# Prompt tokens alone through the seven products, sample tokens through plain products in a bank of their own

## The chip, the cores and the metric

The kernel runs as one launch on one core of a Trainium2 chip. The metric is the device time of that launch in microseconds (us). Before the change it was measured three times: the median is 2774.99 us. A difference of about 0.2%, some 5.5 us, is the least that such a measurement can tell from no change.

## The reference, cut to what matters

One step of a two-layer encoder runs for 1024 prompt tokens and for 8 sample streams of 16 tokens, 1152 tokens in all, in fp32. Model width is 1024 and the channel mixer is 2 x 2816 wide. The part that the change touches is a product of all tokens with a weight matrix, in three places: the up-projection of both layers' channel mixers, and the keys that the second layer's attention shares.

```python
def conv_ffn(h, prev, w_up, conv_w, conv_b, w_down):
    u = h @ w_up                        # 1152 x 1024 times 1024 x 5632
    ...                                 # causal convolution of width 3 over positions
    a, g = jnp.split(y, 2, axis=-1)
    out = (jax.nn.gelu(g) * a) @ w_down
...
kv = ((x * (1 + sc_kv) + sh_kv) @ w_kv_b).reshape(B, T, 2, N_HEADS_B, HEAD_DIM)
```

## The kernel before, in words

Tokens lie along the free dimension of the transposed activations H: nine tiles of 128 tokens, tile 8 holding the samples. Each fp32 operand is split into two parts that TensorE takes in its fp32r format: hi is a cast by ScalarE (ACT) and lo is the rest, a subtraction by VectorE (DVE). The method is `split`, whose cast is at L180 and whose subtraction is at L191. A product of two split operands takes three matmuls per 128-deep slice: lo x hi, hi x lo and hi x hi.

The up-projection of a layer is made in 22 pairs of 128 columns (an "a" block and its gate "g"). The first two pairs of a layer are plain: 24 matmuls per block of about 384 tokens. The other 20 pairs, and four pairs of key columns between the layers, go through `products`, a Strassen-Winograd scheme: a 2 x 2 block product in seven block products, not eight. The token halves are the two 64-token halves of each tile, the depth halves are rows 0-511 and 512-1023, the column halves are the "a" and the "g" block. GpSimd (POOL) makes the sums of weights (L1174 to L1177); `tsums` makes the sums of token blocks once per stage (POOL L1133 and DVE L1134 and L1135, then splits), for all nine tiles, into areas that are 576 = 9 x 64 tokens wide. The names of these areas in the profile are xa, x2r and, for the fourth sum in the key stage, wh and wl.

Each of the seven products is 128 columns x 576 half tokens, cut by `NB` into 320 and 256 tokens in two neighbouring banks of PSUM (the accumulator, 512 fp32 per partition and bank): 12 matmuls with 320 moving columns and 12 with 256 (L1226), 168 in a pair. In a matmul the weight part is the stationary operand, loaded anew for each one (PEld in the profile, as many as matmuls); the tokens move. Products are read out by ACT or DVE at L1185, L1187 and L1194, then added into the rows ua and ug of the pair, and the convolution and the gate follow (`conv_row`, `conv_row_psum`, `gated`). The products of a pair accumulate in three groups of banks: 11 and 21 in group 0; 2, 3 and 4 in group 1; 1 and 22 in group 2. A product that continues a group has to wait until the one before has been read out.

The order of the products is (11, 2, 21, 3, 1, 4, 22). It is (11, 21, 22, 2, 3, 1, 4) in the first pair of a stage, since 11, 21 and 22 need no token sums, and (11, 2, 3, 1, 4, 21, 22) in the last pair of keys. Split weights live in a ring of half slots: eight in layer 0, six in layer 1, three in the key stage. A scheduler orders the instructions of each engine from the written order and the dependencies; it moves whole groups of matmuls ahead where it expects an operand to be late. In layer 0 small matmuls of the modulation (`ada`, L237) run between products. After the second layer's pairs come the down-projections (L1476 in layer 0, L1600 in layer 1) and, elsewhere, products of tokens as the stationary operand (`mmX`, L322).

On-chip memory is laid out by pools in this order: H, the weight slots wh and wl, ws, F, a small area C of 1840 fp32 per partition, then X1 (xa), X2 (x2r) and w0 (w0r). 1840 x 4 bytes is no multiple of 256, all other sizes are. So xa, x2r and w0r start 192 bytes past a multiple of 256, while H, wh and wl start at one.

Of the kernel before, what the change touches and what calls it, by code (L numbers as in the profile page):

```python
# [10 lines left out]
F32 = mybir.dt.float32  # L11
# [24 lines left out]
NPL = 2  # L36
# [69 lines left out]
class Trunk:  # L106
    def __init__(self, ctx, tc, I, O):
# [4 lines left out]
        nc = self.nc  # L112
        mem = ctx.enter_context(tc.tile_pool(name="mem", bufs=1))
# [9 lines left out]
        ws = mem.tile([128, 2, 1024], F32, name="ws")  # L123
# [715 lines left out]
    def kv(self, hmring):  # L839
        nc, I, O, H, F = self.nc, self.I, self.O, self.H, self.F  # L840
# [3 lines left out]

        def T1(p, ks, n):
            m = NB[n][3] - NB[n][2]
            if ks.start < 3:
                return body[p][:, 0:1728].rearrange("p (k n) -> p k n", k=3)[:, ks, NB[n][2] : NB[n][3]]
            x = self.wslots[1][p][:, 512 : 512 + m] if n else body[p][:, 1728 : 1728 + m]
            return x.unsqueeze(1)  # L850

        T1S = F[:, 6180:8484].rearrange("p (k t i) -> p k t i", k=4, i=64)
        TT = self.tviews() + [T1]
        p1s = [F[:, 8484:8804], F[:, 8804:9060]]
# [29 lines left out]
        w = vload(0, self.wslots)  # L884
# [3 lines left out]
        for t in order:  # L888
            vtile(0, t, w, banks.next())
        self.tsums(raws, order, T1S, TT)  # L890

# [9 lines left out]

        sub = Ring(self.subslots(self.wslots[0:2]).items[0:3])
        narrow = self.ws
        wide = Ring(narrow.items + [F[:, o : o + 1024] for o in (3876, 4900)])
        for m in range(4):
            sa, sg = wide.next(), wide.next()
            nc.sync.dma_start(sa, I["wk1"][2 * m])
            nc.sync.dma_start(sg, I["wk1"][2 * m + 1])
            ua, ug = us.next(), us.next()

            def after(i, q, m=m, ug=ug):
                if q == 4:
                    kout(2 * m + 1, ug)

            self.products(sa, sg, ua, ug, S, p1s, sub, TT, after, {0: "first", 3: "last"}.get(m))
            kout(2 * m, ua)
# [206 lines left out]
    def tsums(self, ring, order, T1S, TT):  # L1123
        nc = self.nc
        E = nc.vector if len(TT) == 4 else nc.gpsimd
        for t in order:
            s = ring.next()
            nc.sync.dma_start(s, self.hD[t])
            s4 = s.rearrange("p (c h i) -> p c h i", h=2, i=64)
            b11, b12, b21, b22 = s4[:, 0:4, 0], s4[:, 0:4, 1], s4[:, 4:8, 0], s4[:, 4:8, 1]  # L1130
            x1 = T1S[:, :, t, :]
            E.tensor_sub(x1, b12, b11)
            E.tensor_sub(b12, b22, b12)  # L1133
            nc.vector.tensor_sub(b22, b22, x1)  # L1134
            nc.vector.tensor_sub(b21, b21, b22)  # L1135
            c = slice(64 * t, 64 * t + 64)
            for src, (hi, lo) in zip((b22, b12, b21), TT):
                self.split(src, hi[:, :, c], lo[:, :, c], "a", "v")
            if len(TT) == 4:
                n = t // 5  # L1140
                c = slice(64 * t - 320 * n, 64 * t - 320 * n + 64)
                for ks in (slice(0, 3), slice(3, 4)):
                    hi, lo = (TT[3](p, ks, n)[:, :, c] for p in range(2))
                    self.split(T1S[:, ks, t, :], hi, lo, "a", "v")
        if len(TT) == 3:
            H5 = self.H.rearrange("p a c (t h i) -> p a c t h i", h=2, i=64)
            self.split(T1S, H5[:, 0, 0:4, :, 1, :], H5[:, 1, 0:4, :, 1, :], "a", "v")
# [6 lines left out]
    def products(self, sa, sg, ua, ug, S, p1s, sub, TT, after, when=None):  # L1154
        nc = self.nc
        H5 = self.H.rearrange("p a c (t h i) -> p a c t h i", h=2, i=64)

        def operand(q):
            if q in (2, 3, 4):
                t = TT[q - 2]  # L1160
                return lambda p, k, n: t[p][:, k, NB[n][2] : NB[n][3]]
            if q == 1 and len(TT) == 4:
                return lambda p, k, n: TT[3](p, slice(k, k + 1), n)[:, 0, :]
            c0, h = {11: (0, 0), 21: (4, 0), 22: (4, 1), 1: (0, 1)}[q]
            return lambda p, k, n: H5[:, p, c0 + k, NB[n][0] : NB[n][1], h, :]

        def halves(u, h, n):
            v = u[:, 2 + NB[n][0] * 128 : 2 + NB[n][1] * 128]
            return v.rearrange("p (t h i) -> p t h i", h=2, i=64)[:, :, h, :]

# [8 lines left out]
        def read(d, a, ps, n):  # L1179
            def v(x):  # L1180
                x = x[:, 0 : NB[n][3] - NB[n][2]]
                return x.rearrange("p (t i) -> p t i", i=64)

            if a is None:
                nc.scalar.copy(d, v(ps))  # L1185
            else:
                nc.vector.tensor_add(d, v(ps), a if len(a.shape) == 3 else v(a))  # L1187

        def evict(q, ps, n):
            p1 = p1s[n]  # L1190
            a0, a1, g0, g1 = (halves(u, h, n) for u in (ua, ug) for h in range(2))
            early = when == "first"
            if q == 11:
                nc.scalar.copy(p1, ps[:, 0 : NB[n][3] - NB[n][2]])  # L1194
            elif q == 21:
                read(a0, None, ps, n)
            elif q == 22:
                d = a1 if not early else p1
                read(a1, d, ps, n)
            elif q == 2:  # L1200
                d = a1 if early else p1
                read(a1, d, ps, n)
            elif q == 3:
                read(g1, p1, ps, n)
            elif q == 4:
                read(g0, p1, ps, n)
            else:
                read(g1, g1, ps, n)
                if early:
                    read(a1, a1, ps, n)  # L1210

# [3 lines left out]
        for i, q in enumerate(order):  # L1215
            w = sub.next()
            self.split(src[q], *w, "a", "v")
            x = operand(q)
            start = q in (11, 2, 1) or (q == 22 and when == "first")
            for n in range(2):  # L1220
                m = NB[n][3] - NB[n][2]
                ps = self.bank(2 * group[q] + n)
                c = 0
                for a, p in ((1, 0), (0, 1), (0, 0)):
                    for k in range(4):
                        self.pairmm = nc.tensor.matmul(  # L1226
                            ps[:, 0:m],
                            w[a][:, k * 128 : k * 128 + 128],
                            x(p, k, n),
                            start=start and c == 0,  # L1230
                            stop=c == 11,
                            skip_group_check=True,
                        ).ins
                        c += 1
                evict(q, ps, n)
            after(i, q)
# [4 lines left out]
    def ffn(self, l, xsrc, xdst, affs):  # L1241
# [21 lines left out]
        S1, S2, S3 = [F[:, o : o + 512] for o in (0, 512, 1024)]  # L1263
        p1s = [F[:, 9724:10044], F[:, 10044:10300]]
        T1S = F[:, 2706 : 2706 + 2304].rearrange("p (k t i) -> p k t i", k=4, i=64)
# [4 lines left out]
        cb, sb = Ring([6, 7]), Ring([1, 3, 5])  # L1270
        UB = ((0, 384), (380, 388), (764, 388))
# [48 lines left out]
        def conv_row_psum(u, j, gg, y):  # L1320
# [4 lines left out]
                x.rearrange("p (s q) -> p s q", q=16)  # L1325
                for x in (self.bank(sb.next())[:, 320:448], y[:, 1024:1152], u[:, 1026:1154])
            )
# [61 lines left out]
        def spair(j):  # L1389
# [18 lines left out]

            self.products(sa, sg, ua, ug, (S1, S2, S3), p1s, sub, TT, after, "first" if j == NPL else None)
            ya = yact if l else ys.next()  # L1410
# [10 lines left out]
        if l == 0:  # L1421
            self.bg = [self.ada(g, 7, wide) for g in (3, 4, 5, 6)]
        self.tsums(Ring([F[:, 1536:2560], F[:, 8700:9724], F[:, 11644:12668]]), (0, 1, 2, 3, 4, 8, 5, 6, 7), T1S, TT)
        for u in us.items:
# [632 lines left out]
```

## Time and profile before

| | us |
|---|---|
| median of three runs (lowest to highest) | 2774.99 (2771.91 to 2775.78) |
| the profiled execution's own time | 2778.73 |
| its span from the first to the last instruction | 2776.9 |
| TensorE matmul (PE) busy | 2656.2 (96%) |
| VectorE (DVE) busy | 1916.0 (69%) |
| ScalarE (ACT) busy | 1348.0 (49%) |
| GpSimd (POOL) busy | 1065.7 (38%) |

The 44 pairs run at 532 to 1013 us (layer 0), 1368 to 1466 us (keys) and 2042 to 2503 us (layer 1). In the profile PE is the matmul, PEld the load of a matmul's stationary operand. A matmul's recorded time runs from its start to the end of its results, so neighbours overlap. What a matmul costs in a stream is the distance from its start to the next start: in the timeline, where equal neighbours are merged into one row with their count, it is the start of the next row less the start of this one, divided by the count. A row's second column is the time from its first start to its last end.

### The profile page before, as it was taken

To read this page: it belongs to the slowest core of one execution; us is meant where nothing else is said; L and a number is where in the kernel's file an instruction comes from. 1 tells how busy PE (TensorE), PEld (TensorE's weight loads), DVE (VectorE), ACT (ScalarE), POOL (GpSimd) and SP (SyncE) were. 2 spreads that over 40 slices of the span, in tenths; PEclk is the share of its full clock that TensorE was granted. 3 is DMA by queue.
4 is the path that set the end of the run, shared out by engine and by line. 5 is a ranking of instruction groups with operands and counts; after the bars stand their busy time and mean duration, and the time that the engine had idled before them with its cause. 6 is when DMAs were issued, how large, how long until landed. Compare 5 with 4: busy or idle time off the path is not lost.

```text
span 2776.9 us, 47111 instructions
## 1 busy us (share of the span) xinstructions
PE 2656.2 (96%) x17266; PEld 2345.9 (84%) x17266; DVE 1916.0 (69%) x3836; ACT 1348.0 (49%) x2777; POOL 1065.7 (38%) x775
## 2 busy tenths in 40 slices
PE   7999889999999999999999999989999999999997
PEld 5987768989999998888898888867899999997776
DVE  4376767776666684767754667766787777785669
ACT  3475723433334343443536666662454445454454
POOL 3132623444434357664220121242466656632101
PEclk9999999999999999999999999989999999999999
DMA  7756434464444446765757457773544443347564
GB/s 289 236 162 193 145 103 167 163 236 148 139 158 147 147 135 220 240 217 182 277 192 263 121 155 195 213 213 115 176 143 173 144 138 135 136 148 246 189 221 155
DMA packets 229527, 498.27 MB, mean 179 GB/s; under 512 B 37456, under 2 KB 99232, under 8 KB 229296
## 3 DMA queue, kind: packets, MB, share of 16 engines
q1 hardware_dynamic: 229296, 495.27, 54.6%
q8 instruction: 136, 2.23, 0.3%
q14 instruction: 95, 0.78, 0.1%
HBM read 378.15 MB, written 126.47 MB: 182 GB/s over the span
## 4 chain that ended last, share of the span: by engine, by line
PE 38%; DVE 6%; DMA 4%; ACT 2%; issue 1%; POOL 0%; SPq 0%; DVEq 0%; ACTq 0%; POOLq 0%
PE PS L1226 18%; PE PS L1600 5%; PE PS L322 5%; PE PS L309 4%; PE PS L605 2%; PE PS L583 2%; DMA xa<-actD 1%; PE PS L554 1%; DVE xa L191 1%; DVE F L521 1%; DVE wl L191 1%; PE PS L557 1%; DMA xa<-actS 1%; PE PS L732 0%; DMA wl<-wT 0%
## 5 line engine op out<-in xcount | busy, mean ns | idle before, releaser
L1226 PE MATMUL PS<-H,wh 128*128 128x256 f32 (+1 forms) x2288 | 355.8, 296 | 0.0
L1187 DVE TENSOR_TENSOR F<-PS,F 128x256 f32<-128x256 f32 (+1 forms) x446 | 197.9, 453 | 182.1 <-PE PS L1226 172.7
L1226 PEld LDWEIGHTS PS<-H,wh 128*128 128x128 f32 x2288 | 322.6, 190 | 0.4 <-issue 0.4
L180 ACT CAST wh<-F 128x512 fp32r<-128x512 f32 (+3 forms) x241 | 147.7, 624 | 212.5 <-PE PS L1226 105.5
L191 DVE TENSOR_TENSOR wl<-F,wh 128x512 fp32r<-128x512 f32 (+2 forms) x225 | 213.4, 960 | 40.6 <-ACT wh L180 38.4
L1226 PE MATMUL PS<-H,wl 128*128 128x256 f32 (+1 forms) x1144 | 202.0, 297 | 6.2 <-ACT F L1194 6.2
L1600 PE MATMUL PS<-wh,xa 128*128 128x512 f32 x584 | 187.8, 398 | 14.6 <-ACT wh L180 7.6
L1226 PEld LDWEIGHTS PS<-H,wl 128*128 128x128 f32 x1144 | 168.6, 189 | 12.1 <-ACT F L1194 6.4
L1226 PE MATMUL PS<-xa,wh 128*128 128x320 f32 (+1 forms) x1152 | 175.2, 293 | 0.0
L180 ACT CAST xa<-xa 128x384 fp32r<-128x384 f32 (+2 forms) x143 | 85.8, 604 | 176.0 <-DMA xa<-actD 149.6
L1226 PEld LDWEIGHTS PS<-xa,wh 128*128 128x128 f32 x1152 | 159.0, 188 | 0.4 <-issue 0.4
L1469 DVE TENSOR_TENSOR xa<-xa 128x384 fp32r<-128x384 f32 x66 | 94.4, 1441 | 83.4 <-ACT xa L180 83.3
L1600 PEld LDWEIGHTS PS<-wh,xa 128*128 128x128 f32 x584 | 110.3, 190 | 44.3 <-ACT wh L180 11.8
L180 ACT CAST wh<-ws 128x512 fp32r<-128x512 f32 (+1 forms) x131 | 95.5, 736 | 101.4 <-PE PS L1226 44.2
L643 POOL TENSOR_TENSOR F<-F,x2r 64x512 f32<-64x512 f32 x62 | 79.4, 1280 | 165.9 <-DVE F L619 149.3
L1346 POOL TENSOR_TENSOR F<-F 128x1152 f32<-128x1152 f32 x44 | 124.1, 2820 | 43.9 <-DVE F L1339 18.1
L322 PE MATMUL PS<-xa,H 128*128 128x512 f32 x504 | 133.5, 406 | 6.2 <-ACT xa L180 3.3
L309 PE MATMUL PS<-H,w0r 128*128 128x384 f32 (+1 forms) x720 | 136.1, 340 | 0.0
L1275 DVE SCALAR_TENSOR_TENSOR F<-F 128x1024 f32<-128x1024 f32 (+2 forms) x160 | 132.1, 876 | 3.1 <-ACT F L1314 2.1
L309 PE MATMUL PS<-H,wh 128*128 128x384 f32 (+1 forms) x672 | 131.1, 338 | 0.0
L583 PE MATMUL PS<-C,F 128*128 128x128 f32 x720 | 112.7, 281 | 14.5 <-DVE wh L590 5.8
L309 PEld LDWEIGHTS PS<-H,w0r 128*128 128x128 f32 x720 | 123.2, 188 | 2.8 <-issue 1.1
(354 smaller groups left out, 6883.8 us busy)
## 6 DMA issues: line engine op xcount, KB each, us to landing
ws<-in_adaw_dram SPq DMA_DIRECT2D x64, 512.0 KB
ws<-in_wup_dram SPq DMA_DIRECT2D x49, 512.0 KB
F<-in_adaw_dram SPq DMA_DIRECT2D x48, 512.0 KB
F<-in_wup_dram SPq DMA_DIRECT2D x39, 512.0 KB
actD<-F SPq DMA_DIRECT2D x33, 576.0 KB
ws<-in_wdn_dram SPq DMA_DIRECT2D x33, 512.0 KB
F<-in_wdn_dram SPq DMA_DIRECT2D x33, 512.0 KB
xa<-kH SPq DMA_DIRECT2D x60, 256.0 KB
```

The lines of the kernel that those rows point to most:

```text
L180: nc.scalar.copy(out, in_)
L191: self.eng(el).tensor_sub(lo, src, hi.bitcast(F32))
L309: mm = self.nc.tensor.matmul(out[:, 0:n], w[a][:, k * 128 : k * 128 + 128], H[:, p, k, s0 : s0 + n], start=i == 0, stop=i == 23)
L322: self.nc.tensor.matmul(out[:, 0:n], H[:, p, j * kn + k, t0 : t0 + 128], w[a][:, k * n : k * n + n], start=i == 0, stop=i == 23,)
L583: nc.tensor.transpose(t[:, n * 128 : n * 128 + 128], p[:, (kt - k0) * 128 : (kt - k0) * 128 + 128], self.ident)
L643: self.eng("v" if last else "p").tensor_mul(on[r, q], on[r, q], rb[r, :])
L1187: nc.vector.tensor_add(d, v(ps), a if len(a.shape) == 3 else v(a))
L1226: self.pairmm = nc.tensor.matmul(ps[:, 0:m], w[a][:, k * 128 : k * 128 + 128], x(p, k, n), start=start and c == 0, stop=c == 11, skip_grou ...
L1275: nc.vector.scalar_tensor_tensor(o, u, cw[:, cc, i : i + 1], o, op0=ALU.mult, op1=ALU.add)
L1346: nc.gpsimd.tensor_mul(yg, yg, ya)
L1469: nc.vector.tensor_sub(lo, raw, hi.bitcast(F32))
L1600: self.downmm = nc.tensor.matmul(ps, a[p][:, i * 128 : i * 128 + 128], w[q], start=first and c == 0, stop=last and c == 2, skip_group_chec ...
```

## The change

The seven products now take the 1024 prompt tokens alone: 512 half tokens, a full bank, in 12 matmuls per product in place of 24. The areas of token sums are 512 wide, `tsums` runs over eight tiles, and the groups are banks 0, 1 and 2. The 128 sample tokens get their two output blocks by plain products: 8 depth slices x 3 matmuls for each of "a" and "g", 48 matmuls with 128 moving columns per pair, in bank 3 or 4 by turns. They use the split weights that the products have anyway (11, 21 and 4); only the plain block a21 has to be split in addition, before POOL overwrites it with a sum. ACT copies the two sample blocks out. The key stage's ring has four half slots in place of three. C grows by 16 fp32 per partition, so that xa, x2r and w0r start at a multiple of 256 bytes as H, wh and wl do.

```diff
-NB = ((0, 5, 0, 320), (5, 9, 320, 576))
...
-        C = mem.tile([128, 1840], F32, name="C")
+        C = mem.tile([128, 1856], F32, name="C")
...
-        sub = Ring(self.subslots(self.wslots[0:2]).items[0:3])
+        sub = self.subslots(self.wslots[0:2])
+        sbanks = Ring([3, 4])
...
-        TT = [(X1[:, 0:2304], X1[:, 2304:4608]), (X1[:, 4608:6912], X1[:, 6912:9216]), (X2[:, 0:2304], X2[:, 2304:4608])]
+        TT = [[x[:, o : o + 2048] for o in (i, i + 2048)] for x, i in ((X1, 0), (X1, 4096), (X2, 0))]
...
         E.tensor_sub(S3, a11, a21)
+        ws = sub.next()
+        self.split(a21, *ws, "a", "v")
         E.tensor_sub(a21, a12, S2)
...
+        def sample(b, w, c0, start=False):
+            n = slice(128 * b, 128 * b + 128)
+            i = 0
+            for a, p in ((1, 0), (0, 1), (0, 0)):
+                for k in range(4):
+                    nc.tensor.matmul(
+                        su[:, n],
+                        w[a][:, k * 128 : k * 128 + 128],
+                        H[:, p, c0 + k, 1024:1152],
+                        start=start and i == 0,
+                        stop=b in done and i == 11,
+                        skip_group_check=True,
+                    )
+                    i += 1
+            if b in done:
+                nc.scalar.copy((ua, ug)[b][:, 1026:1154], su[:, n])
+            done.add(b)
...
-            for n in range(2):
-                m = NB[n][3] - NB[n][2]
-                ps = self.bank(2 * group[q] + n)
-                c = 0
-                for a, p in ((1, 0), (0, 1), (0, 0)):
-                    for k in range(4):
-                        self.pairmm = nc.tensor.matmul(
-                            ps[:, 0:m],
-                            w[a][:, k * 128 : k * 128 + 128],
-                            x(p, k, n),
...
+            ps = self.bank(group[q])
+            c = 0
+            for a, p in ((1, 0), (0, 1), (0, 0)):
+                for k in range(4):
+                    self.pairmm = nc.tensor.matmul(
+                        ps,
+                        w[a][:, k * 128 : k * 128 + 128],
+                        x(p, k),
...
+            evict(q, ps)
+            if q == 11:
+                sample(0, w, 0, True)
+                sample(1, ws, 0)
+            elif q in (21, 4):
+                sample(q % 3, w, 4)
```

TensorE's order in a steady pair of layer 0. In the rows "H,w0r" means: tokens from H move, the weight slot w0r is loaded; L237 is the modulation. Before, products 11, 2 and 21 of one pair:

```order
L1226 MATMUL PS<-H,w0r 128x320 x12
L1226 MATMUL PS<-H,w0r 128x256 x12
L237 MATMUL PS<-F,C 32x256 x4
L1226 MATMUL PS<-xa,w0r 128x320 x12
L1226 MATMUL PS<-xa,w0r 128x256 x12
L1226 MATMUL PS<-H,wl 128x320 x4
L1226 MATMUL PS<-H,wh 128x320 x8
L1226 MATMUL PS<-H,wl 128x256 x4
L1226 MATMUL PS<-H,wh 128x256 x8
```

And of the changed kernel, products 11, 2 and 21 of such a pair (L1231 are the products, L1206 the samples):

```order
L1231 MATMUL PS<-H,w0r 128x512 x12
L1206 MATMUL PS<-H,w0r 128x128 x24
L1231 MATMUL PS<-xa,wl 128x512 x4
L1231 MATMUL PS<-xa,wh 128x512 x8
L1231 MATMUL PS<-H,wl 128x512 x4
L1231 MATMUL PS<-H,wh 128x512 x8
L1206 MATMUL PS<-H,wl 128x128 x4
L1206 MATMUL PS<-H,wh 128x128 x8
```

A run of 24 sample matmuls now stands behind product 11 and a run of 12 behind product 21; the last 12 stand around product 4. Over the whole program the 2112 sample matmuls stand in 172 runs.

The first pair of layer 1 on TensorE, behind the last plain block (128x388). Before:

```order
L309 MATMUL PS<-H,wh 128x388 x16
L1226 MATMUL PS<-H,wl 128x320 x4
L1226 MATMUL PS<-H,wh 128x320 x8
L1226 MATMUL PS<-H,wl 128x256 x4
L1226 MATMUL PS<-H,wh 128x256 x8
L1226 MATMUL PS<-H,wl 128x320 x4
L1226 MATMUL PS<-H,wh 128x320 x8
```

And changed:

```order
L308 MATMUL PS<-H,wh 128x388 x16
L1231 MATMUL PS<-H,wl 128x512 x4
L1231 MATMUL PS<-H,wh 128x512 x8
L1206 MATMUL PS<-H,wl 128x128 x4
L1206 MATMUL PS<-H,wh 128x128 x8
L1206 MATMUL PS<-H,wl 128x128 x4
L1206 MATMUL PS<-H,wh 128x128 x8
L1231 MATMUL PS<-xa,wl 128x512 x4
L1231 MATMUL PS<-xa,wh 128x512 x8
L1231 MATMUL PS<-H,wl 128x512 x4
L1231 MATMUL PS<-H,wh 128x512 x8
```

Product 11 was followed by another product over H in the same banks; now 24 sample matmuls and a product over token sums (xa) stand between the two.

More of the change, by code (lines that the diff above doesn't have):

```diff
@@ L843, in kv @@
         body = [self.w2[a][:, 1:3].rearrange("p s c -> p (s c)") for a in range(2)]
-        def T1(p, ks, n):
-            m = NB[n][3] - NB[n][2]
[L847 to L854, printed above, removed]
+        T1S = F[:, 6180:8228].rearrange("p (k t i) -> p k t i", k=4, i=64)
+        TT = self.tviews() + [[x.rearrange("p (k n) -> p k n", k=4) for x in body]]
+        p1 = F[:, 8484:8996]
         hl = [F[:, o : o + 1024].bitcast(F32R) for o in (9060, 10084)]
@@ L889, in kv @@
             vtile(0, t, w, banks.next())
-        self.tsums(raws, order, T1S, TT)
+        self.tsums(raws, [t for t in order if t < 8], T1S, TT)
         def kout(c, u):
@@ L913, in after @@
                     kout(2 * m + 1, ug)
-            self.products(sa, sg, ua, ug, S, p1s, sub, TT, after, {0: "first", 3: "last"}.get(m))
+            self.products(sa, sg, ua, ug, S, p1, sub, TT, sbanks.next(), after, {0: "first", 3: "last"}.get(m))
             kout(2 * m, ua)
@@ L1139, in tsums, with products, halves @@
             if len(TT) == 4:
[L1140 to L1144, printed above, removed]
+                hi, lo = TT[3]
+                self.split(T1S[:, :, t, :], hi[:, :, c], lo[:, :, c], "a", "v")
         if len(TT) == 3:
             H5 = self.H.rearrange("p a c (t h i) -> p a c t h i", h=2, i=64)
-            self.split(T1S, H5[:, 0, 0:4, :, 1, :], H5[:, 1, 0:4, :, 1, :], "a", "v")
+            self.split(T1S, H5[:, 0, 0:4, 0:8, 1, :], H5[:, 1, 0:4, 0:8, 1, :], "a", "v")
     def tviews(self):
         X1, X2 = self.X1, self.X2
-        TT = [(X1[:, 0:2304], X1[:, 2304:4608]), (X1[:, 4608:6912], X1[:, 6912:9216]), (X2[:, 0:2304], X2[:, 2304:4608])]
+        TT = [[x[:, o : o + 2048] for o in (i, i + 2048)] for x, i in ((X1, 0), (X1, 4096), (X2, 0))]
         return [[x.rearrange("p (k n) -> p k n", k=4) for x in t] for t in TT]
-    def products(self, sa, sg, ua, ug, S, p1s, sub, TT, after, when=None):
+    def products(self, sa, sg, ua, ug, S, p1, sub, TT, sbank, after, when=None):
         nc = self.nc
-        H5 = self.H.rearrange("p a c (t h i) -> p a c t h i", h=2, i=64)
+        H = self.H
+        H5 = H.rearrange("p a c (t h i) -> p a c t h i", h=2, i=64)
         def operand(q):
[L1159 to L1163, printed above, removed]
+            if q in (2, 3, 4) or (q == 1 and len(TT) == 4):
+                t = TT[(q - 2) % 4]
+                return lambda p, k: t[p][:, k, :]
             c0, h = {11: (0, 0), 21: (4, 0), 22: (4, 1), 1: (0, 1)}[q]
[L1165 to L1169, printed above, removed]
+            return lambda p, k: H5[:, p, c0 + k, 0:8, h, :]
+        def halves(u, h):
+            return u[:, 2:1026].rearrange("p (t h i) -> p t h i", h=2, i=64)[:, :, h, :]
         S1, S2, S3 = S
@@ L1325, in conv_row_psum @@
                 x.rearrange("p (s q) -> p s q", q=16)
-                for x in (self.bank(sb.next())[:, 320:448], y[:, 1024:1152], u[:, 1026:1154])
+                for x in (self.bank(sb.next())[:, 0:128], y[:, 1024:1152], u[:, 1026:1154])
             )
@@ L1407, in after @@
                     row(ug, j, 1, y[0])
-            self.products(sa, sg, ua, ug, (S1, S2, S3), p1s, sub, TT, after, "first" if j == NPL else None)
+            self.products(sa, sg, ua, ug, (S1, S2, S3), p1, sub, TT, sbanks.next(), after, "first" if j == NPL else None)
             ya = yact if l else ys.next()
@@ L1422, in ffn @@
             self.bg = [self.ada(g, 7, wide) for g in (3, 4, 5, 6)]
[L1423 removed]
+        self.tsums(Ring([F[:, 1536:2560], F[:, 8700:9724], F[:, 11644:12668]]), range(8), T1S, TT)
         for u in us.items:
```

46 lines of the change are left out of this document (21 added, 25 removed).

## The prediction

> **What bounds the kernel now.** First the page, for the engine that has no time to spare; then the windows of the stretch in which pair follows pair; then the timeline of TensorE, for what one matmul costs from start to start.
>
> ```profile
> span 2776.9 us, 47111 instructions
> PE 2656.2 (96%) x17266; PEld 2345.9 (84%) x17266; DVE 1916.0 (69%) x3836; ACT 1348.0 (49%) x2777; POOL 1065.7 (38%) x775
> ...
> PE PS L1226 18%; PE PS L1600 5%; PE PS L322 5%; PE PS L309 4%; PE PS L605 2%; PE PS L583 2%; DMA xa<-actD 1%; PE PS L554 1%; DVE xa L191 1%; DVE F L521 1%; DVE wl L191 1%; PE PS L557 1%; DMA xa<-actS 1%; PE PS L732 0%; DMA wl<-wT 0%
> ```
>
> TensorE is busy for 96% of the span, and L1226, the seven products, is the largest line of the chain that ends last. The windows (us, then busy time of PE, PEld, DVE, ACT, POOL) say whether anybody is waited for there. This stretch of layer 1 holds 16 pairs:
>
> ```profile
> 2117.60:2472.40 354.80, 354.79 (x2690) 354.57 (x2689) 269.86 (x469) 179.43 (x356) 223.93 (x170) 1.00 0.40 140
> ```
>
> PE has no idle time at clock 1.00; DVE has a quarter of it free, ACT half. A pair takes 354.80 / 16 = 22.18 us, and only PE's stream sets it. Layer 0 shows a pair without modulation, of which these are the start, three products and the next start:
>
> ```profile
> 968.52 0.83 PE L1226 MATMUL PS<-H,wl 128*128 128x320 f32 x4
> ...
> 971.80 3.35 PE L1226 MATMUL PS<-xa,w0r 128*128 128x320 f32 x24
> 974.99 3.34 PE L1226 MATMUL PS<-H,w0r 128*128 128x320 f32 x24
> 978.16 0.75 PE L1226 MATMUL PS<-xa,wl 128*128 128x320 f32 x4
> 978.75 1.34 PE L1226 MATMUL PS<-xa,wh 128*128 128x320 f32 x8
> 979.92 0.62 PE L1226 MATMUL PS<-xa,wl 128*128 128x256 f32 x4
> ...
> 990.80 0.75 PE L1226 MATMUL PS<-H,wl 128*128 128x320 f32 x4
> ```
>
> The pair takes 990.80 - 968.52 = 22.28 us, a product 3.17 to 3.19. A matmul of 320 columns costs 146 ns ((979.92 - 978.75) / 8), so one of 256 costs (3.18 - 12 x 0.146) / 12 = 119 ns. I take 22.2 us per pair, 44 times.
>
> **The products at 512 columns.** No product runs so in this trace, but other lines do:
>
> ```profile
> 1266.88 8.32 PE L1476 MATMUL PS<-x2r,xa 128*128 128x512 f32 x36
> 1275.04 0.40 PE L1476 MATMUL PS<-wh,xa 128*128 128x512 f32 x1
> ...
> 1945.24 5.76 PE L322 MATMUL PS<-xa,H 128*128 128x512 f32 x24
> 1950.84 0.39 PE L322 MATMUL PS<-wh,H 128*128 128x512 f32 x1
> ```
>
> Where both operands lie in areas with the same remainder modulo 256 bytes (x2r and xa), a matmul costs 8.16 / 36 = 227 ns; where they differ by 192 (xa and H), 5.60 / 24 = 233 ns. After the change all are alike. I take 228, a little over the better row for changes between areas; the bounds are 227 and 233. A product becomes 12 x 0.228 = 2.74 us, seven of them 19.15 us, against 22.2: a gain of 3.05 us per pair.
>
> **The samples at 128 columns.** 48 matmuls per pair, each with its own weight load. The rows with such matmuls in fp32r are in the first layer's attention (L605, four of them, then L309), and as transposes at L1039:
>
> ```profile
> 130.83 0.44 PE L605 MATMUL PS<-wh,xa 128*128 128x128 f32 x3
> 130.89 0.50 PE L605 MATMUL PS<-wh,xa 128*128 128x128 f32 x3
> 130.94 0.30 PEld L605 LDWEIGHTS PS<-wh,xa 128*128 128x128 f32 x2
> 131.23 0.56 PE L309 MATMUL PS<-H,w0r 128*128 128x384 f32 x2
> ...
> 1939.30 1.04 PE L1039 MATMUL PS<-C,F 128*128 128x128 f32 x8
> 1940.10 0.71 PE L322 MATMUL PS<-xa,H 128*128 128x512 f32 x2
> ```
>
> The two L605 rows are overlapping views of one run. The first matmul, behind a long one, hands over after 130.89 - 130.83 = 0.06 us. From there it is three steps to 131.23, 0.113 us each. The weight load of a step starts at 130.94, only after the matmul before it had started at 130.89: with 128 columns there is no long matmul in whose shadow the load can lie, so load and stream alternate. The eight transposes have the same step, 0.8 us for seven steps and a handover. I take 111 ns inside a run and 58 for the first of a run. The bounds are 58 (every load hidden) and 115.
>
> Samples of a pair in four runs: 44 x 0.111 + 4 x 0.058 = 5.12 us. A pair becomes 19.15 + 5.12 = 24.27 us, 2.07 more than 22.2. Times 44: **+91 us**. In columns alone the change is nearly even (7 x 12 x 576 = 48384 before, 7 x 12 x 512 + 48 x 128 = 49152 after); the loss is that 48 short matmuls cost their weight load too.
>
> The Trainium skill has another price ("TensorE: Matmul & The Clock Gate", Back-to-back issue gap): a sustained stream of load and matmul is said to take about 81 ns each at 128 columns and about 131 at 512. By these figures a pair would take 84 x 0.131 + 48 x 0.081 = 14.9 us, an estimate; the 227 ns of the row above already speaks against the second figure.
>
> **First pairs of the stages.** Before the 44 pairs run freely, PE waits for the token sums (its idle time stands in brackets with what ended it):
>
> ```profile
> 541.15 4.75 PE L1226 MATMUL PS<-H,w0r 128*128 128x320 f32 x24 [2.42 <-ACT F L1194]
> ...
> 1379.33 0.85 PE L1226 MATMUL PS<-xa,w0r 128*128 128x320 f32 x4 [1.07 <-ACT xa L180]
> 1382.09 2.89 PE L1226 MATMUL PS<-xa,w0r 128*128 128x320 f32 x20 [1.92 <-DVE xa L191]
> 1385.79 0.85 PE L1226 MATMUL PS<-wh,wl 128*128 128x320 f32 x4 [0.81 <-DVE F L1187]
> 1394.27 3.46 PE L1226 MATMUL PS<-x2r,w0r 128*128 128x320 f32 x24 [1.84 <-DVE F L1187]
> ...
> 2051.54 1.43 PE L1226 MATMUL PS<-H,wl 128*128 128x320 f32 x4 [6.18 <-ACT F L1194]
> 2052.78 2.33 PE L1226 MATMUL PS<-H,wh 128*128 128x320 f32 x8
> ```
>
> In both layers product 21 waits until ACT has read out 11, and ACT comes to that late, behind this cast of the last sum:
>
> ```profile
> 2047.46 2.11 ACT L180 CAST H<-F 128x2304 fp32r<-128x2304 f32 x1
> ```
>
> After the wait PE also runs slow for a while (2.33 us for eight matmuls that take 1.34 elsewhere). Behind product 11 there now stand 24 sample matmuls, 2.6 us of work that needs no sums, and in layer 1 a product over xa; the cast has 2048 columns, not 2304, and one tile of nine less is summed. I take layer 0's wait and its slow matmuls as gone (2.4 + 1.4), 7 us of layer 1's 6.2 + 2.3, and 3 us of the keys' 5.6. Together **-14 us**, between -4 and -20. What is late next there is the DVE, whose splits of the sums the product over xa awaits.
>
> **The places modulo 256 bytes.** Lines outside the pairs with 512 columns and unlike areas gain at most 233 - 227 = 6 ns each:
>
> ```profile
> L322 PE MATMUL PS<-xa,H 128*128 128x512 f32 x504 | 133.5, 406 | 6.2 <-ACT xa L180 3.3 <-DVE xa L191 1.5 <-DVE F L521 1.1
> L322 PE MATMUL PS<-w0r,H 128*128 128x512 f32 x162 | 44.0, 406 | 3.0 <-DVE F L1118 3.0
> L1600 PE MATMUL PS<-wh,xa 128*128 128x512 f32 x584 | 187.8, 398 | 14.6 <-ACT wh L180 7.6 <-DVE F L1729 2.8 <-DVE xa L191 2.3
> ```
>
> (504 + 162) x 6 ns = 4 us, and some 4 us more for the x2r rows of L322 and for L1600 and L1476, where the step already lies nearer to the good one. **-8 us**, between 0 and -12.
>
> **What costs nothing.** ACT, DVE and POOL work beside PE. The durations for it, from the same 16 pairs:
>
> ```profile
> L191 DVE TENSOR_TENSOR wl<-F,wh 128x512 fp32r<-128x512 f32 x81 | 78.1, 968 | 8.9 <-ACT wh L180 7.9 <-POOL F L1360 0.3 <-DMA ws<-in_wup_dram 0.2
> L1275 DVE SCALAR_TENSOR_TENSOR PS<-F,PS 128x512 f32<-128x512 f32 x65 | 48.5, 750 | 9.1 <-ACT PS L1337 9.1
> L1187 DVE TENSOR_TENSOR F<-PS,F 128x320 f32<-128x320 f32 x80 | 38.9, 486 | 10.8 <-PE PS L1226 8.9
> L1187 DVE TENSOR_TENSOR F<-PS,F 128x256 f32<-128x256 f32 x81 | 34.1, 420 | 39.8 <-PE PS L1226 36.6 <-ACT F L1194 3.0
> L180 ACT CAST wh<-F 128x512 fp32r<-128x512 f32 x81 | 50.1, 621 | 56.9 <-PE PS L1226 56.3
> ```
>
> DVE gets one split more, 0.97 us, and reads five products in one piece (0.75, the nearest row) in place of two (0.49 + 0.42): 0.97 - 5 x 0.16 = +0.2 us on 16.9 per pair. ACT gets a cast (0.62) and two sample copies (under 0.5 each), on 11.2. Both stay under the longer pair's 24 us. POOL's last weight sum now waits for the split of a21, with the next pair's sums and the gate's product queued behind it; it feeds product 22, seventh in order, some 18 us later. One bank per group means that the read-out (0.75 us and a handover) no longer hides under the other half of the same product; but between 2 and 3 stands 21, between 3 and 4 stands 1, each 2.74 us. Where that cover failed, one such wait per pair would cost 0.9 x 44 = 40 us. On SP's queue nothing is added and one tile load of nine per stage goes; weight loads get more time per pair.
>
> **Sum.** +91 - 14 - 8 = +69 us. The profiled execution took 2778.73 us, so 2848 by its own time; the median of the runs lies 3.7 lower, 2775 + 69 = **2844 us**.
>
> **Rivals.** (A) *Faster: the loads hide.* If PE loads ahead throughout, each sample matmul costs the 58 ns of a run's first: 48 x 0.058 = 2.8 us, a pair 21.95, -0.25 x 44 = -11, with -14 - 8 in all -33: 2742 us. It decides below (22.2 - 19.15) / 48 = 64 ns per sample matmul. For it: the first step of L605. Against it: every later one, and the transposes. 5%. (B) *Half of the loads hide*, 85 ns on average between 58 and 111: 4.1 us, a pair 23.2, +1.03 x 44 = +45, in all +23: 2798 us. Beside it stands the skill's 81 ns for 128 columns, the same page and section; no row here shows such a step. 6%. (C) *Read-outs come late*: the one-bank wait above once per pair, or ACT held up at the sample copies behind the next casts: +40 on the forecast, 2884 us. Against it: the order and ACT's free half. 7%. (D) *The longer matmul gives nothing beyond what 233 ns gives*: 84 x 5 ns x 44 = +18, 2862; within the range.
>
> **Chances and range.** The forecast, with D, has 82%. Its bounds: the 512 step -4 to +18, the sample step -15 (104 ns, if some runs are broken up) to +8, first pairs -6 to +10, places -4 to +8. Taken together 2815 to 2880; the range for 8 in 10 reaches down to B: 2802 to 2880. About 0.2%, 5.5 us, is what a measurement can tell from no change: faster 0.05 (A), the same 0.02 (between A and B), slower 0.93.
>
> **What would show it.** In the changed profile L1231 should step by 227 to 233 ns and L1206 by about 111 inside a run; a steady pair of layer 1 should take 24.3 us with PE busy throughout; the wait of 6.18 us at product 21 of layer 1 should be mostly gone. It is wrong if L1206 steps by 60 ns, if PE shows idle time before L1231 inside the steady pairs, or if a pair takes 22 us.

## The result, and the profile after

| | before | after |
|---|---|---|
| median, us (lowest to highest, four runs each) | 2775.38 (2771.91 to 2775.78) | 2865.91 (2862.35 to 2869.55) |
| the profiled execution's own time, us | 2778.73 | 2869.55 |
| its span, us | 2776.9 | 2867.8 |

The ratio is 1.0329, 95% interval 1.031 to 1.0348: the changed kernel is slower by some 90 us. The forecast was 2844, with a range of 2802 to 2880. (Of the four runs of before, three are those known ahead.) The page of the changed kernel, for the engine that sets the time:

```profile
span 2867.8 us, 43709 instructions
PE 2755.7 (96%) x15682; PEld 2299.8 (80%) x15682; DVE 1904.1 (66%) x3630; ACT 1377.0 (48%) x2802; POOL 1068.3 (37%) x771
...
PE PS L1231 28%; PE PS L321 11%; PE PS L1206 7%; PE PS L308 7%; PE PS L1486 7%; PE PS L1610 4%; PE PS L604 2%; PE PS L582 2%; PE PS L236 2%; PE PS L553 1%; DMA ws<-in_adaw_dram 1%; DMA F<-xd 1%; PE PS L295 1%; PE PS L556 1%; PE PS L731 1%
```

TensorE has 1584 matmuls fewer, is busy for the same 96% of the span, and is busy for 99.5 us longer. The samples' line, L1206, has entered the chain of work that ended last with 7%. Nobody else has become the bound. Steady pairs of layer 1 in the windows view (us; busy time of PE, PEld, DVE, ACT, POOL; granted clock), 13 of them:

```profile
2199.97:2519.77 319.80, 319.80 (x1717) 274.62 (x1716) 227.65 (x326) 151.86 (x300) 186.59 (x139) 1.00 0.36 127
```

A pair takes 319.80 / 13 = 24.60 us in place of 22.18, with PE busy throughout. The same view of the two kernels gives the lengths of the stages. Each is cut where the last matmul of a stage is done; where a few matmuls of the next stage stand ahead of it, they are counted with the next. (Layer 0's pairs end at 1036 us in the kernel before, not at 1013.)

| stage | before | after | difference |
|---|---|---|---|
| up to layer 0's pairs | 532.3 | 531.6 | -0.7 |
| 20 pairs of layer 0 | 503.8 | 552.9 | +49.1 |
| down-projection 0 and what follows | 332.4 | 339.7 | +7.3 |
| 4 pairs of keys | 96.9 | 102.6 | +5.7 |
| attention of layer 1 | 576.6 | 573.3 | -3.3 |
| 20 pairs of layer 1 | 452.6 | 493.5 | +40.9 |
| down-projection 1 and the end | 282.3 | 274.2 | -8.1 |
| span | 2776.9 | 2867.8 | +90.9 |

The pairs hold +95.7 us, and all the rest together -4.8. Inside a steady pair, TensorE's timeline of the changed kernel (start, length, line, operands, count) shows product 11's 24 sample matmuls, product 2, product 21 and its 12 samples:

```profile
2178.11 0.56 PE L1206 MATMUL PS<-H,wl 128*128 128x128 f32 x4
2178.50 1.06 PE L1206 MATMUL PS<-H,wh 128*128 128x128 f32 x8
2179.40 0.61 PE L1206 MATMUL PS<-H,wl 128*128 128x128 f32 x4
2179.85 1.06 PE L1206 MATMUL PS<-H,wh 128*128 128x128 f32 x8
2180.74 1.16 PE L1231 MATMUL PS<-xa,wl 128*128 128x512 f32 x4
2181.74 2.00 PE L1231 MATMUL PS<-xa,wh 128*128 128x512 f32 x8
2183.57 1.07 PE L1231 MATMUL PS<-H,wl 128*128 128x512 f32 x4
2184.48 1.98 PE L1231 MATMUL PS<-H,wh 128*128 128x512 f32 x8
2186.29 0.56 PE L1206 MATMUL PS<-H,wl 128*128 128x128 f32 x4
2186.68 1.06 PE L1206 MATMUL PS<-H,wh 128*128 128x128 f32 x8
2187.58 1.16 PE L1231 MATMUL PS<-xa,wl 128*128 128x512 f32 x4
```

A long matmul steps by (2186.29 - 2184.48) / 8 = 226 ns, as forecast. A sample matmul inside a run steps by (2180.74 - 2179.85) / 8 = 111 ns, as forecast too, and the first of a run is short: (2178.50 - 2178.11) / 4 = 97 ns on average for four with the first among them. What the forecast didn't have stands behind the run: the first four long matmuls take 2181.74 - 2180.74 = 1.00 us, where four others (2183.57 to 2184.48) take 0.91. A run gets back at its end what it saved at its head, so 24 samples cost 2.63 + 0.09 = 2.72 us, 113 ns each.

Now the first pairs of the stages, where the kernel before waited 6.18 us in layer 1, 2.42 in layer 0 and 5.64 in the quoted rows of the keys. These are the waits there in the timeline of after, with one at the end of layer 0 (idle time in brackets, with what ended it):

```profile
541.08 2.08 PE L1231 MATMUL PS<-H,wl 128*128 128x512 f32 x4 [3.59 <-ACT F L1182]
...
567.02 1.40 PE L1231 MATMUL PS<-x2r,wl 128*128 128x512 f32 x4 [1.30 <-DVE F L1176]
...
1021.31 1.67 PE L1231 MATMUL PS<-xa,wl 128*128 128x512 f32 x4 [1.76 <-DVE F L1176]
...
1448.73 2.08 PE L1231 MATMUL PS<-x2r,wl 128*128 128x512 f32 x4 [2.65 <-DVE F L1176]
...
2117.93 1.18 PE L1231 MATMUL PS<-H,wl 128*128 128x512 f32 x4 [1.32 <-DVE F L1176]
```

Layer 1's wait is mostly gone and the keys' are halved. Layer 0's has grown, and the wait at 1021.31, near the end of layer 0's pairs, is new. Behind most of these waits TensorE's clock is down for some 3 to 5 us, as the windows of after show at the keys' wait:

```profile
1448.73:1452.10 3.37, 3.37 (x8) 2.68 (x9) 2.22 (x3) 0.00 (x0) 0.47 (x1) 0.53 0.15 51
```

Eight matmuls take 3.37 us at a granted clock of 0.53. The down-projection of layer 0 now starts with two waits as well, in the timeline of TensorE and then of ACT:

```profile
1089.17 1.66 PE L1486 MATMUL PS<-wh,xa 128*128 128x512 f32 x6 [1.06 <-ACT wh L179]
...
1094.31 0.80 PE L1486 MATMUL PS<-wl,xa 128*128 128x512 f32 x1 [2.81 <-POOL wl L190]
```

```profile
1087.13 1.05 ACT L179 CAST xa<-ws 128x1024 fp32r<-128x1024 f32 x1 [3.16 <-DMA ws<-in_wdn_dram]
```

A weight tile lands late there, the cast of it starts late, and POOL's splits come late behind the cast. Behind the second wait the granted clock is 0.50 for 5.3 us.

### The profile page after: what moved, and what is told of

It reads as the page before. It is cut to its first block, busy times and chain, and to the rows that moved or that the text cites. A ratio compares the mean times of both kernels' runs of the same rounds, so it can differ in the third digit from the quotient of the medians.

```text
span 2867.8 us, 43709 instructions
## 1 busy us (share of the span) xinstructions
PE 2755.7 (96%) x15682; PEld 2299.8 (80%) x15682; DVE 1904.1 (66%) x3630; ACT 1377.0 (48%) x2802; POOL 1068.3 (37%) x771
## 4 chain that ended last, share of the span: by engine, by line
PE 78%; DMA 9%; DVE 7%; ACT 3%; issue 2%; POOL 1%; SPq 0%; DVEq 0%; ACTq 0%; POOLq 0%
PE PS L1231 28%; PE PS L321 11%; PE PS L1206 7%; PE PS L308 7%; PE PS L1486 7%; PE PS L1610 4%; PE PS L604 2%; PE PS L582 2%; PE PS L236 2%; PE PS L553 1%; DMA ws<-in_adaw_dram 1%; DMA F<-xd 1%; PE PS L295 1%; PE PS L556 1%; PE PS L731 1%
## 5 line engine op out<-in xcount | busy, mean ns | idle before, releaser
L1231 PE MATMUL PS<-H,wh 128*128 128x512 f32 x1184 | 294.1, 390 | 0.0
L1176 DVE TENSOR_TENSOR F<-PS,F 128x512 f32<-128x512 f32 x223 | 153.1, 688 | 192.3 <-PE PS L1231 191.5
L190 DVE TENSOR_TENSOR wl<-F,wh 128x512 fp32r<-128x512 f32 (+1 forms) x244 | 231.3, 965 | 69.8 <-ACT wh L179 68.4
L1231 PEld LDWEIGHTS PS<-H,wh 128*128 128x128 f32 x1184 | 222.6, 188 | 47.6 <-issue 0.4
L179 ACT CAST wh<-F 128x512 fp32r<-128x512 f32 (+2 forms) x260 | 162.8, 640 | 161.1 <-PE PS L1231 99.1
L1231 PE MATMUL PS<-xa,wh 128*128 128x512 f32 x672 | 168.5, 393 | 0.0
L1231 PE MATMUL PS<-H,wl 128*128 128x512 f32 x592 | 163.0, 397 | 4.9 <-ACT F L1182 3.6
L1231 PEld LDWEIGHTS PS<-xa,wh 128*128 128x128 f32 x672 | 127.1, 189 | 29.2
L1206 PE MATMUL PS<-H,wh 128*128 128x128 f32 x1016 | 138.4, 273 | 0.0
L1206 PEld LDWEIGHTS PS<-H,wh 128*128 128x128 f32 x1016 | 127.9, 192 | 2.3
L1231 PEld LDWEIGHTS PS<-H,wl 128*128 128x128 f32 x592 | 108.3, 189 | 26.7 <-ACT F L1182 3.7
```

The costliest lines, as they stand in the source:

```text
L179: nc.scalar.copy(out, in_)
L190: self.eng(el).tensor_sub(lo, src, hi.bitcast(F32))
L1206: nc.tensor.matmul(su[:, n], w[a][:, k * 128 : k * 128 + 128], H[:, p, c0 + k, 1024:1152], start=start and i == 0, stop=b in done and i == 11,
L1231: self.pairmm = nc.tensor.matmul(ps, w[a][:, k * 128 : k * 128 + 128], x(p, k), start=start and c == 0, stop=c == 11, skip_group_check=Tru ...
```

## The experiments

All kernels are edits of the changed kernel, but for one that is an edit of the kernel before. Ratios are against the kernel before, on the same chip.

### One sample matmul in twelve

```diff
-            for a, p in ((1, 0), (0, 1), (0, 0)):
-                for k in range(4):
+            for a, p in ((0, 0),):
+                for k in range(1):
...
```

> The changed kernel with only one of the twelve matmuls of each sample block: 4 sample matmuls per pair in place of 48, so the sample tokens' up-projections and keys are not computed. Theory (each sample matmul costs about 113 ns of TensorE's time, its weight load included): 44 x 44 x 0.113 = 219 us less, 2866 - 219 = 2647 us, a steady pair of layer 1 19.7 us. Rival 1 (a sample matmul costs its stream, 58 ns, and the rest of the loss comes from later read-outs and new waits): 2866 - 112 = 2754 us. Rival 2 (DVE or ACT become the bound of the shorter pair): between, with PE idle in the steady pairs.

Measured: 2708.94 us (2700.22 to 2716.22), ratio 0.9767 (0.9736 to 0.9797). Pairs in which nobody waits take 19.55 us, 5.05 less than 24.60, for 44 matmuls: 115 ns each. So 48 of them cost 5.5 us, and the seven products alone 24.60 - 5.5 = 19.1. But the time fell by 157 us where 44 x 5.05 = 222 had gone. The waits of this kernel's TensorE (sum in us, times, longest):

```profile
PE PS L1231 <- DVE F L1176: 37.7, 29, 4.7
...
PE PS L1231 <- DVE wl L190: 9.2, 11, 2.3
```

In the changed kernel the first of these rows holds 7.0 us in 4 waits, and the second is not there: 40 of the missing 65 us are new waits for DVE, and the rest was not taken apart. At under 20 us per pair DVE's read-outs and splits come late. That a sample matmul has the price of the theory holds; that the whole time follows does not, since the samples also cover DVE. The time lies where rival 2 had it, between 2647 and 2754, with TensorE idle in some of the steady pairs.

### 256 moving columns per sample matmul

```diff
-                        H[:, p, c0 + k, 1024:1152],
+                        H[:, p, c0 + k, 896:1152],
...
```

> The changed kernel with sample matmuls of 256 moving columns (tile 7's 128 tokens and the samples), of which the last 128 are read out as before; the extra columns are computed and thrown away. Theory (load of the next operand runs beside the stream of a matmul, and a step can't be shorter than the load): the step goes from 113 to 118 or 120 ns, 2112 x 6 ns = +13 us, 2879 us. Rival (load and stream of these matmuls follow one another, so that 128 columns more cost 53 ns more each): 2112 x 53 ns = +112 us, 2978 us.

Measured: 2881.12 us (2877.99 to 2886.84), ratio 1.039 (1.0366 to 1.0413). In the timeline, a run of 24 and the first long matmuls behind it:

```profile
2213.15 0.64 PE L1206 MATMUL PS<-H,wl 128*128 128x256 f32 x4
2213.63 1.12 PE L1206 MATMUL PS<-H,wh 128*128 128x256 f32 x8
2214.59 0.64 PE L1206 MATMUL PS<-H,wl 128*128 128x256 f32 x4
2215.07 1.12 PE L1206 MATMUL PS<-H,wh 128*128 128x256 f32 x8
2216.03 1.09 PE L1231 MATMUL PS<-xa,wl 128*128 128x512 f32 x4
2216.96 1.98 PE L1231 MATMUL PS<-xa,wh 128*128 128x512 f32 x8
```

The run takes 2.88 us, 120 ns each, and the four long ones behind it 0.93. With twice the columns a pair takes 24.88 us, 0.28 / 48 = 6 ns more per sample matmul. Had load and stream been added up, it would have been 57 ns, what 128 of the 512 columns of a long step take. So 128 columns stand on a floor that 256 columns just exceed.

### 64 moving columns per sample matmul

```diff
-                        H[:, p, c0 + k, 1024:1152],
+                        H[:, p, c0 + k, 1024:1088],
...
```

> The changed kernel with sample matmuls of 64 moving columns: the second half of the samples isn't computed and the first half is copied in its place. Theory (the step can't be shorter than the weight load, about 111 ns): the step stays at 110 to 113 ns, 2866 us, between 2856 and 2874. Rival (the prediction's picture: load and stream follow one another, 59 + 52 ns, so half the columns save 26 ns each): 2112 x 26 ns = -55 us, 2811 us.

Measured: 2874.15 us (2866.52 to 2883.24), ratio 1.0363 (1.0342 to 1.0385): not less than the changed kernel's 1.0329. Timeline of a run of 24:

```profile
2215.55 0.53 PE L1206 MATMUL PS<-H,wl 128*128 128x64 f32 x4
2215.91 1.06 PE L1206 MATMUL PS<-H,wh 128*128 128x64 f32 x8
2216.81 0.61 PE L1206 MATMUL PS<-H,wl 128*128 128x64 f32 x4
2217.26 1.06 PE L1206 MATMUL PS<-H,wh 128*128 128x64 f32 x8
2218.15 1.18 PE L1232 MATMUL PS<-xa,wl 128*128 128x512 f32 x4
```

Half the columns, and still 2.60 us for 24, with (2218.15 - 2217.26) / 8 = 111 ns inside the run. A pair takes 24.51 us, 0.09 less than in the changed kernel; the whole time is no shorter, at the upper end of what was expected. The rival, in which the stream's share halves, is out.

### 64 stationary columns per sample matmul

```diff
-                        su[:, n],
-                        w[a][:, k * 128 : k * 128 + 128],
+                        su[0:64, n],
+                        w[a][:, k * 128 : k * 128 + 64],
...
```

> The changed kernel, with 64 of the 128 stationary columns in each sample matmul; the moving side keeps its 128 columns. The other 64 rows of the samples' up-projection and gate are not computed (the 64 rows are copied twice), so ACT copies in four pieces of 64 rows in place of two of 128. What it tells apart is what makes the floor of some 111 ns per sample matmul, which fewer moving columns did not lower. Theory: the weight load, which takes a time by its columns; with half of them a step falls to about 60 ns (the 58 ns that the first sample matmul of a run takes), and a steady pair of layer 1 from 24.60 to 24.60 - 48 x 0.05 = 22.2 us. The whole time would fall by up to 44 x 2.4 = 105 us to about 2761 us, but as VectorE then has less cover (with one sample matmul in twelve some pairs waited for it), 2770 to 2810. Rival: the floor is a fixed cost of any matmul that follows a short one, whatever it loads; the pair stays at 24.5 to 24.6 and the time at 2866 us (2860 to 2880).

Measured: 2771.08 us (2768.26 to 2778.51), ratio 1.0007 (0.9991 to 1.0023). Timeline of a run of 24, and the windows of 15 pairs:

```profile
2139.20 0.40 PE L1206 MATMUL PS<-H,wl 128*64 128x128 f32 x4
2139.44 0.64 PE L1206 MATMUL PS<-H,wh 128*64 128x128 f32 x8
2139.92 0.40 PE L1206 MATMUL PS<-H,wl 128*64 128x128 f32 x4
2140.16 0.64 PE L1206 MATMUL PS<-H,wh 128*64 128x128 f32 x8
2140.64 1.14 PE L1232 MATMUL PS<-xa,wl 128*128 128x512 f32 x4
```

```profile
2136.50:2470.20 333.70, 333.70 (x1981) 279.70 (x1980) 278.52 (x378) 191.33 (x377) 216.03 (x160) 1.00 0.38 135
```

With half the columns to load, the step falls from 111 to 1.44 / 24 = 60 ns, and a pair to 333.70 / 15 = 22.25 us. So the load sets the floor of 111 ns: fewer moving columns change nothing, fewer stationary ones bring it down. Half the stationary columns also mean half the rows of results, but the records of the loads themselves are shorter by 57 ns. Here they are in this kernel (shortest, median and longest in ns) and on the page of the changed one (busy time, mean ns):

```profile
L1206 PEld LDWEIGHTS PS<-H,wh x1016: 133/135/137, 532.4 to 2486.9; 128*64 128x64 f32 x170
```

```profile
L1206 PEld LDWEIGHTS PS<-H,wh 128*128 128x128 f32 x1016 | 127.9, 192 | 2.3
```

The Trainium skill ("TensorE: Matmul & The Clock Gate", LDWEIGHTS) puts a load at its columns divided by 1.2, 107 ns for 128 and 53 for 64. The measured 111 agrees with the first. The 60 shows only that a load of 64 columns takes no longer than that, since the stream of 128 moving columns also takes some 60, half of the 120 ns for 256. The 81 ns that the Trainium skill gives for a step at 128 columns ("TensorE: Matmul & The Clock Gate", Back-to-back issue gap) don't agree with the 111. Halving these loads takes away as much as the change had cost: with the step at 60 ns the kernel is level with the one before. DVE's cover holds at this pace, its row of waits is 9.5 us.

### Sample matmuls between the long ones

```diff
+                    yield
...
+                    for g in gens:
+                        next(g)
```

Each sample matmul is written behind a product's matmul, in place of in runs. In the trace product 11's 24 stand so, in twos; those of 21 and 4 stand partly alone and partly still in runs of 9 to 12.

> The changed kernel with the sample matmuls written one or two at a time between the product matmuls that use the same weight slice, so that most stand alone between matmuls of 512 columns. Theory (a sample matmul costs 113 to 119 ns wherever it stands, since what it saves at its head the next long matmul pays): 2866 us, between 2856 and 2880. Rival (a load hides in the shadow of a neighbouring long matmul, so a single short one costs 58 ns): about half to all of the samples gain 55 ns, 2750 to 2810 us.

Measured: 2878.91 us (2870.36 to 2891.6), ratio 1.0385 (1.0348 to 1.0421). The timeline in product 11:

```profile
2315.45 0.45 PE L1234 MATMUL PS<-H,wh 128*128 128x512 f32 x1
2315.74 0.33 PE L1206 MATMUL PS<-H,wh 128*128 128x128 f32 x2
2315.91 0.45 PE L1234 MATMUL PS<-H,wh 128*128 128x512 f32 x1
2316.20 0.33 PE L1206 MATMUL PS<-H,wh 128*128 128x128 f32 x2
```

From long matmul to long matmul it takes 0.46 us for one long and two short ones: 0.23 for the two above the long one's 0.227, as much as in a run. The pair that holds these rows takes 24.60 us, the same as in runs. Loads don't hide under the neighbour: the long matmul (2315.45 to 2315.74) steps by 290 ns, not 227, and only one of the short ones starts early for it. Other pairs take more, the next one 26.5 us, since a read-out comes late there, as in this row of the same timeline:

```profile
2352.55 1.19 PE L1234 MATMUL PS<-xa,wl 128*128 128x512 f32 x4 [1.11 <-DVE F L1176]
```

The rival is out.

### Products as two halves of 256 columns

```diff
+            for n in range(2):
...
-                        ps,
+                        ps[:, 256 * n : 256 * n + 256],
```

> The changed kernel with each prompt product as two matmuls of 256 columns into the two halves of its bank, in place of one of 512; samples as in the changed kernel. Theory (a matmul costs its columns and 6 to 14 ns, so joining two saves little): 2 x 117 to 2 x 120 in place of 231 ns, 3 to 9 ns x 3696 = +11 to +33 us, 2877 to 2899 us. Rival (the longer matmul is what shortened the products by 3 us per pair): +132 us, 2998 us.

Measured: 2902.04 us (2899.12 to 2906.82), ratio 1.0466 (1.0447 to 1.0485). The windows of 15 pairs:

```profile
2188.92:2571.42 382.50, 382.50 (x3243) 382.50 (x3242) 250.25 (x376) 176.79 (x346) 205.80 (x157) 1.00 0.36 122
```

And two rows of a product, in the timeline:

```profile
2304.05 1.12 PE L1234 MATMUL PS<-xa,wh 128*128 128x256 f32 x8
2305.01 0.64 PE L1234 MATMUL PS<-xa,wl 128*128 128x256 f32 x4
```

A pair takes 25.50 us, and a matmul of 256 columns 0.96 / 8 = 120 ns. That splits the change in two. From 320 and 256 to 256 and 256 columns the products go from 22.2 to 168 x 0.120 = 20.2 us. Joined to 512 they go to 19.1: by the pairs the wide matmul itself gives 25.50 - 24.60 = 0.90 us, 40 us in 44 pairs, and the whole time differs by 36. The samples, 5.5 us, cost more than the 3.1 of both together. The rival of +132 us is out; the theory was too low, with 33 us and 2899 at most, since joining two saves 2 x 120 - 227 = 13 ns and not 3 to 9.

### The places undone, and the places alone

The changed kernel with C at its old size, and the kernel before with C at the new one (the same line the other way round):

```diff
-        C = mem.tile([128, 1856], F32, name="C")
+        C = mem.tile([128, 1840], F32, name="C")
```

> The changed kernel with C at 1840 again: xa, x2r and w0r start 192 bytes past a multiple of 256, as before the change. Theory (a 512-column step is 227 ns where both operands lie alike modulo 256 bytes and 229 to 233 ns where not): product rows over xa and x2r with wh or wl go from about 230 to 233 or more, 1056 x 3 to 6 ns = 3 to 6 us; the rows of the other lines go back to their steps of before, 4 to 10 us. In all +7 to +16 us, 2873 to 2882 us. Rival (the places do nothing): 2866 us with equal steps.

Measured: 2881.04 us (2876.64 to 2885.19), ratio 1.0387 (1.0371 to 1.0402), within what was expected.

> The kernel before with C at 1856 and nothing else: all areas alike modulo 256 bytes. Theory: lines with 512 columns gain 2 to 6 ns a step, -8 to -12 us; the pairs' 256-column matmuls over xa and x2r with wh and wl step by 113 ns while unlike and by 120 where alike, so 1296 of them lose up to 7 ns, +5 to +9 us. In all -7 to +1 us, 2768 to 2776 us, most likely 2771. Rival (alike is better at every width): -12 us or more, 2763 us.

Measured: 2774.23 us (2759.31 to 2782.88, eleven runs), ratio 1.0000 (0.9984 to 1.0017). Two groups of this kernel (busy time, mean ns of one), and the first of them in the kernel before:

```profile
L1226 PE MATMUL PS<-xa,wh 128*128 128x256 f32 x576 | 81.3, 283 | 0.0
...
L322 PE MATMUL PS<-xa,H 128*128 128x512 f32 x504 | 129.3, 398 | 6.2 <-ACT xa L180 3.3 <-DVE xa L191 1.5 <-DVE F L521 1.1
```

```profile
L1226 PE MATMUL PS<-xa,wh 128*128 128x256 f32 x576 | 78.0, 277 | 0.0
```

In the changed kernel the places are worth (1.0387 - 1.0329) x 2774 = 16 us; the two intervals leave some 9 to 23. A steady pair of layer 1 takes 24.71 us with the old places and 24.60 with the new ones, 5 us in 44 pairs. In the kernel before they are worth nothing that can be measured: L322 gains 133.5 - 129.3 = 4.2 us, and the products' half of 256 columns loses 3.3 in this group alone. In these groups a matmul of 512 columns is faster with both operands at like places, and one of 256 slower. Not every group follows: the x2r rows of L322 (512 columns) take 38.5 us before and 38.6 with like places. For the second kernel this comes out at the upper end of what was expected: no gain.

## Why the prediction was right, and where its sizes were off

**The sign and its cause were right.** The change loses because 48 short matmuls cost their weight load: the kernel whose sample loads are half as long is level with the one before. The break-even that the prediction worked out, 64 ns per sample matmul, stands between that kernel's 60 and the measured 113.

**The 512 step was right.** 228 ns were taken, and 19.15 us for seven products; the pairs of the first experiment give 19.1.

**The samples' term was 0.4 us too small per pair.** The step that failed is "58 for the first of a run", counted as a saving for four runs. It is one, but the first long matmuls behind a run give it back (0.09 us in the quoted rows; the product's first step is some 60 ns longer). A run of 24 costs 113 ns each, one of 12 costs (1.29 + 0.09) / 12 = 115. By the first experiment 48 cost 5.5 us, not 5.12. A pair became 24.60, not 24.27, and 44 x 0.33 = 14.5 us is the largest part of the miss of 22. The first pairs hold some 4 us of it and the rest of the program 3.

**The picture behind the 111 ns was wrong.** "Load and stream alternate" would make the step shorter with fewer moving columns, and longer by the whole stream with more. It did neither with 64 and 256. Up to 128 moving columns the step is the load's alone. The 111 ns held because they were read from rows with matmuls of this shape, not because of the picture, which two runs refuted.

**First pairs: -14 was forecast, about -10 came.** The pairs' stages grew by 95.7 us, and 44 steady pairs at 2.4 make 105.6. By stage, with 2.4 for each pair, layer 1 gained 7.1 us and the keys 3.9, close to the 7 and 3 that were forecast. Layer 0 lost 1.1, where a gain of 3.8 was forecast. Layer 1's wait fell from 6.18 to 1.32. Layer 0's was counted as gone and is 3.59. ACT's read-out of product 11 comes behind the same casts at nearly the same time as before (540.45 us, and 540.67 in the kernel before), but TensorE is there sooner: product 11 is 0.45 us shorter, and behind it stand samples of 2.6 us in place of a product of 3.2. The wait at 1021 with its slow matmuls was not foreseen either.

**What is late next is DVE, but not its splits of the sums.** The prediction named these splits. The waits of 2.65 us in the keys and 1.32 in layer 1 are for read-outs (L1176). Each stands on DVE behind the split of a weight, which had waited for ACT's cast (6.65 and 3.18 us). In the keys ACT came to that cast late, behind L927, which had waited 3.64 us for a transfer (hmD).

**Places: -8 was forecast for the lines outside the pairs; these stages give -4.8.** In them stands +7.3 us at the first down-projection, so the others gained 12.1; what of that is the places' was not taken apart line by line. The undone places cost some 16 us in the whole kernel, more than the 8, since they also hold the products over xa and x2r, at 229 in place of 233 ns. The +7.3 stands in the trace as a late weight tile and POOL's late splits behind it (1.06 and 2.81 us of waits, then matmuls at half the clock), and 2.3 us more of waits at L1032. The places don't make it: the changed kernel with the old places waits there too, 0.66 and 3.14 us. The kernel before doesn't, nor do those with the samples spread, with half loads and with one sample matmul in twelve. What makes the tile late stays open.

**The rivals.** A and B fell with the step of 111 ns. C fell too: in layer 1's steady pairs no read-out holds TensorE up (busy for 319.80 of 319.80 us); in the timeline of DVE one takes 0.68 us, less than the 0.75 that were taken. D had 2862 us, nearer to the measured time than the forecast. That is chance: a long matmul steps by 226 to 229 ns, not 233, and even with the old places only three of the seven products of a layer 1 pair step by 233.

**Two slips in the working.** The upper bounds of the range add up to +44, which is 2888 and not 2880; the measured time lies below both. The eight transposes step by some 106 ns (0.80 us less 0.06, by seven), not by the 111 to 113 of the other rows.

## What to carry to other kernels

Count the short matmuls, not their columns: in these formats each one costs its 128-column weight load, 111 to 115 ns, wherever it stands, so work in short matmuls should give up its loads (tokens put beside others under one load) before it gives up columns. A saving at the head of a run is real only if the first step behind the run is counted too. And a layout that suits one width may cost another: here the same 64 bytes more in C gain in groups of 512 columns and lose in groups of 256.

## What the runs showed that was not expected

- The step of a matmul with 64, 128 and 256 moving columns is 111, 111 and 120 ns with 128 stationary columns, and 60 ns with 128 moving and 64 stationary ones.
- Put in twos between long matmuls, short ones cost as much as in a run (0.23 us for two).
- Two matmuls of 256 columns cost 240 ns, one of 512 costs 227: joining them saves 13 ns.
- Unlike places modulo 256 bytes cost 4 ns per step at 512 columns in the products over xa (233, not 229) and gain 6 at 256 (277, not 283, in the mean length of a matmul).
- After the waits of 1.30, 1.76, 2.65, 2.81 and 3.59 us TensorE's matmuls were slow for some 3 to 5 us, at a granted clock of 0.50 to 0.66 in the windows behind them. After 1.32 us in layer 1 four of them took 2118.94 - 2117.93 = 1.01 us, as after any run. The clock was 1.00 there, and also after a wait of 1.60 in the kernel with the spread samples. So the length of the wait alone doesn't decide it; what does was not tried. The row behind the wait of 1.32 us, in the timeline:

```profile
2118.94 1.98 PE L1231 MATMUL PS<-H,wh 128*128 128x512 f32 x8
```
